# Weight splits held behind the residual chain, and three chain operations on another engine, in a two-layer hybrid trunk

## The chip, the cores and the metric

The kernel runs on one core of a Trainium2 chip. TensorE does the matrix products, VectorE and ScalarE the elementwise work, GpSimd some of it and a part of the DMA issues; SyncE (SP) issues the weight transfers. The metric is device time in microseconds of one execution; lower is better. Engine names in profiles: PE is TensorE (PEld its weight load), DVE is VectorE, ACT is ScalarE, POOL is GpSimd, SP is SyncE.

## What is computed

A decoder trunk of two layers on one sequence of 256 rows, 2048 wide, in float32. Each layer adds a normed mixer and a normed SwiGLU to the residual:

```python
def reference(x, mix_norm_pre, mix_norm_post, ffn_norm_pre, ffn_norm_post, ev_w_in, ...):
    h = x
    for layer in range(DEPTH):
        i = layer // 2
        u = rms_norm(h, mix_norm_pre[layer])
        if layer % 2 == 0:
            u = even_mixer(u, ev_w_in[i], ev_conv_w[i], ev_a_log[i], ev_dt_bias[i], ev_onorm[i], ev_w_out[i])
        else:
            u = odd_mixer(u, od_w_in[i], od_w_out[i])
        h = h + rms_norm(u, mix_norm_post[layer])
        u = swiglu(rms_norm(h, ffn_norm_pre[layer]), ffn_w_gate[layer], ffn_w_up[layer], ffn_w_down[layer])
        h = h + rms_norm(u, ffn_norm_post[layer])
    return h
```

`even_mixer` is one input projection, stick-breaking attention on 8 heads and gated DeltaNet on 8 others, and an output projection; `odd_mixer` has block-sparse and dilated attention between its two projections. The SwiGLU is 5632 wide.

## The kernel before

**Products.** The 256 rows are two tiles of 128, t = 0 and t = 1. A float32 product is three products of a reduced type: each operand is split into a high and a low part, and `step` (L271 to L273) adds high x high, high x low and low x high into the same PSUM tile. The activations are held transposed, one pair (high, low) per 512 columns. A step is 256 rows by 512 columns of a weight, with 6 matmuls for each tile.

**Weights.** All weights pass once through the chip. `load_until` (L230 on) issues a step's transfer on SP into one of four `raw` buffers (512 KB each), and `split` makes the parts: ScalarE copies the high one (L221), VectorE subtracts it for the low one (L222). Most steps have two halves of 128x512. A `raw` buffer is free for the next transfer when the splits have read it; the `w` pool holds ten steps. Some steps of the SwiGLU go a shorter way with sums of blocks (`split_sums`, `fast_step`); they aren't touched.

**Phases.** There are six: input projection, output projection and SwiGLU of each layer. In `run_phase` (L328), tile 0 runs up to eight steps ahead of tile 1 at a phase's beginning and end. When tile 0 has done its last step, `end(0)` writes its chain into the program, while TensorE goes on with tile 1's last steps:

- `post_residual` (L461): the factor `prf` from the sums of squares (`rms`, L205, with the power on GpSimd, L192, and L194, L198, L468), then for four column groups x += y * prf (L471) and the next phase's operand y (L475 behind the SwiGLU, L478 behind an output projection), which TensorE transposes (L373) and `split` divides into m tiles (L221, L222 again).
- The norm weights and y were multiplied before that: by L786 behind an output projection, by L731 in `down_chunk` behind the SwiGLU (column groups 0 to 2 on GpSimd, group 3 on VectorE). L722 adds the last product to y.

The chain has a raised priority (LEAD). The order on each engine is set by the scheduler of the language when the program is built, from the written order, priorities and its own estimate of when operands are ready; so the weight splits of the next phase are mixed with the chain on VectorE.

**DeltaNet.** `gdn_core` makes two 128-row blocks for each of two head groups. For each of the four, L1158 scales a product of keys into L, L1160 adds its two halves on GpSimd, and TensorE takes the sum into L1175. L1209 subtracts a state product on GpSimd (in two of the four).

Stages named in the text: A and B, two of the four L1160; F, G and H, the ends of layer 0's output projection, layer 0's SwiGLU and layer 1's output projection.

## Time and profile before

| | |
|---|---|
| Runs, us | 2388.26, 2392.54, 2393.22 (median 2392.54) |
| Profiled execution, us | 2395.03 |
| Its span, us | 2393.3 |
| Mean granted clock of TensorE | 0.99 |
| Busy: PE, PEld, DVE, ACT, POOL | 98%, 84%, 74%, 52%, 9% |

The span runs from the first to the last instruction; the execution's time has 1.7 us around it. The page gives shares over the whole span. With TensorE at 98%, what matters is where it is not busy, which the views by waits and by stretches show. The granted clock is the share of the full 2.4 GHz that TensorE was given; 0.5 is 1.2 GHz. Busy times of a group count overlapping parts of neighbouring instructions twice, so a pitch (start to start) is shorter than a mean duration.

### The profile page before, as it was taken

To read this page: it belongs to the slowest core of one execution; us is meant where nothing else is said; L and a number is where in the kernel's file an instruction comes from. 1 tells how busy PE (TensorE), PEld (TensorE's weight loads), DVE (VectorE), ACT (ScalarE), POOL (GpSimd) and SP (SyncE) were. 2 spreads that over 40 slices of the span, in tenths; PEclk is the share of its full clock that TensorE was granted. 3 is DMA by queue.
4 is the path that set the end of the run, shared out by engine and by line. 5 is a ranking of instruction groups with operands and counts; after the bars stand their busy time and mean duration, and the time that the engine had idled before them with its cause. 6 is when DMAs were issued, how large, how long until landed. Compare 5 with 4: busy or idle time off the path is not lost.

```text
span 2393.3 us, 33293 instructions
## 1 busy us (share of the span) xinstructions
PE 2346.8 (98%) x12235; PEld 2007.9 (84%) x12235; DVE 1760.4 (74%) x2823; ACT 1256.2 (52%) x1975; POOL 218.6 (9%) x269
## 2 busy tenths in 40 slices
PE   9999989999999999999998999999999999999998
PEld 7878877778888888888887888887888888888886
DVE  7775875668868697877867555567886878697885
ACT  6654564555645454544555545455554545454552
POOL 0430361210000000000121000011000000000011
PEclk9999999999999999999999999999999999999999
DMA  7644445365656556565675555576565656666573
GB/s 248 207 145 146 141 141 172 115 225 178 217 177 197 191 194 200 187 217 169 220 253 194 168 175 176 181 231 214 176 226 168 210 180 194 193 194 201 191 264 110
DMA packets 131140, 453.72 MB, mean 190 GB/s; under 512 B 15568, under 2 KB 20944, under 8 KB 130976
## 3 DMA queue, kind: packets, MB, share of 16 engines
q1 hardware_dynamic: 120704, 423.81, 53.9%
q0 software_dynamic: 8112, 26.52, 3.5%
q8 instruction: 96, 1.57, 0.3%
q10 hardware_dynamic: 2160, 1.27, 0.2%
q14 instruction: 68, 0.56, 0.1%
HBM read 443.11 MB, written 8.42 MB: 189 GB/s over the span
## 4 chain that ended last, share of the span: by engine, by line
PE 80%; DVE 3%; DMA 1%; issue 1%; POOL 1%; ACT 1%; DVEq 0%; POOLq 0%; ACTq 0%
PE p L273 11%; PE p L271 11%; PE p L272 11%; PE acc L273 10%; PE acc L271 10%; PE acc L272 10%; PE acc L296 2%; PE acc L297 2%; PE acc L295 2%; PE p L297 2%; PE p L296 2%; PE p L295 2%; DVE w L222 1%; PE p L216 1%; DMA raw<-in_ffn_w_down 1%
## 5 line engine op out<-in xcount | busy, mean ns | idle before, releaser
L222 DVE TENSOR_TENSOR w<-raw,w 128x512 fp32r<-128x512 f32 (+4 forms) x1104 | 987.2, 915 | 432.6 <-ACT w L221 386.6
L221 ACT ACTIVATE w<-raw 128x512 fp32r<-128x512 f32 (+4 forms) x1104 | 844.1, 795 | 832.5 <-PE p L273 313.7
L271 PE MATMUL acc<-w,m 128*128 128x512 f32 (+2 forms) x1582 | 617.4, 391 | 5.5 <-ACT m L224 3.2
L272 PE MATMUL acc<-w,m 128*128 128x512 f32 (+2 forms) x1582 | 616.4, 390 | 0.0
L273 PE MATMUL acc<-w,m 128*128 128x512 f32 (+2 forms) x1582 | 615.3, 390 | 0.8 <-DVE m L222 0.8
L271 PE MATMUL p<-w,m 128*128 128x512 f32 x1146 | 450.0, 393 | 3.6 <-ACT m L221 2.9
L273 PE MATMUL p<-w,m 128*128 128x512 f32 x1146 | 449.9, 393 | 0.0
L272 PE MATMUL p<-w,m 128*128 128x512 f32 x1146 | 449.3, 392 | 0.0
L271 PEld LDWEIGHTS acc<-w,m 128*128 128x128 f32 x1582 | 299.9, 190 | 64.9 <-ACT m L224 3.8
L273 PEld LDWEIGHTS acc<-w,m 128*128 128x128 f32 x1582 | 299.4, 189 | 61.1 <-DVE m L222 1.7
L272 PEld LDWEIGHTS acc<-w,m 128*128 128x128 f32 x1582 | 299.7, 189 | 57.4
L271 PEld LDWEIGHTS p<-w,m 128*128 128x128 f32 x1146 | 216.1, 189 | 48.0 <-ACT m L221 3.3
L273 PEld LDWEIGHTS p<-w,m 128*128 128x128 f32 x1146 | 215.7, 188 | 45.0
L272 PEld LDWEIGHTS p<-w,m 128*128 128x128 f32 x1146 | 215.8, 188 | 44.1
L222 DVE TENSOR_TENSOR w<-sums,w 128x1024 fp32r<-128x1024 f32 x126 | 153.5, 1218 | 3.0 <-ACT w L221 2.9
L221 ACT ACTIVATE w<-sums 128x1024 fp32r<-128x1024 f32 x126 | 132.4, 1051 | 18.8 <-DVE sums L259 18.5
L297 PE MATMUL acc<-w,m 128*128 128x256 f32 x462 | 131.5, 285 | 0.0
L296 PE MATMUL acc<-w,m 128*128 128x256 f32 x462 | 130.7, 283 | 0.0
L295 PE MATMUL acc<-w,m 128*128 128x256 f32 x462 | 130.5, 282 | 0.0
L257 DVE TENSOR_TENSOR sums<-raw 128x512 f32<-128x512 f32 x126 | 86.8, 689 | 51.1 <-DMA raw<-in_ffn_w_gate 25.4
L438 POOL DMA_DIRECT2D m<-in_ffn_norm_post x16 | 8.8, 551 | 1264.0 <-PE p L273 630.4
L297 PE MATMUL p<-w,m 128*128 128x256 f32 x420 | 119.3, 284 | 0.0
(279 smaller groups left out, 2372.1 us busy)
## 6 DMA issues: line engine op xcount, KB each, us to landing
raw<-in_ffn_w_gate SPq DMA_DIRECT2D x176, 512.0 KB, 3.5
raw<-in_ffn_w_up SPq DMA_DIRECT2D x176, 512.0 KB, 4.1
raw<-in_ffn_w_down SPq DMA_DIRECT2D x176, 512.0 KB, 4.5
raw<-in_ev_w_in SPq DMA_DIRECT2D x104, 512.0 KB, 3.5
raw<-in_od_w_in SPq DMA_DIRECT2D x96, 512.0 KB, 3.5
raw<-in_ev_w_out SPq DMA_DIRECT2D x32, 512.0 KB, 4.5
raw<-in_od_w_out SPq DMA_DIRECT2D x32, 512.0 KB, 4.5
xd<-m POOLq DMA_DIRECT2D x24, 256.0 KB, 4.0
```

The costliest lines, as they stand in the source:

```text
L216: self.nc.tensor.transpose(o[:, j * P:(j + 1) * P], src[:, j, :], self.ident)
L221: self.nc.scalar.activation(h, src, AF.Copy)
L222: self.nc.vector.tensor_sub(l, src, h.bitcast(F32))
L257: nc.vector.tensor_sub(t[:, 0:2], b[:, 0:1].broadcast_to([P, 2, 256]), b[:, 1:3])
L271: nc.tensor.matmul(acc, xh, s.wh[:, j], start=(s.first and j == 0), stop=False)
L272: nc.tensor.matmul(acc, xh, s.wl[:, j], start=False, stop=False)
L273: nc.tensor.matmul(acc, xl, s.wh[:, j], start=False, stop=end)
L295: nc.tensor.matmul(acc, xh, s.wh[:, b], start=s.first and i in (0, 2), stop=True, **kw)
L296: nc.tensor.matmul(acc, xh, s.wl[:, b], start=False, stop=True, **kw)
L297: nc.tensor.matmul(acc, xl, s.wh[:, b], start=False, stop=True, **kw)
L438: self.nc.gpsimd.dma_start(out=w, in_=src.broadcast_to([P, 512]))
```

## The change

1. `post_residual` returns its last VectorE operation, and `run_phase` keeps it together with the next four steps (HOLD) whose transfers haven't been issued. When `load_until` comes to these steps, the VectorE half of their splits (L222) is ordered behind that operation; the ScalarE half and the transfer aren't. That happens at the end of layer 0's output projection, layer 0's SwiGLU and layer 1's output projection; the input projections have no such chain, and behind the last SwiGLU no step is left.
2. L731 (column groups 0 to 2), L1160 and L1209 go from GpSimd to VectorE: 12, 4 and 2 instructions.

```diff
@@ -55,6 +57,7 @@
 PSA = 3
 NSP = 3
 LEAD = 500
+HOLD = 4
 PS_FFN = 3
 WARM = 10
 FFN_GROUPS = ((0, 1), (2, 3), (4, 5), (6, 7), (8, 9), (10,))
@@ -154,7 +157,7 @@
         psb = pool("psb", bufs=1, space=PSUM)
         dram = pool("dram", bufs=1, space=bass.MemoryType.DRAM)
         self.mem = Pool(big, "m", NTILES)
-        self.lag = LAG
+        self.lag, self.hold = LAG, None
         self.ps = Pool(psb, "p", NPS)
         self.pa = Pool(psb, "acc", PSA)
         self.cin = Pool(big, "c", 2, (P, 4, P + 3))
@@ -215,11 +218,12 @@
         for j in range(4):
             self.nc.tensor.transpose(o[:, j * P:(j + 1) * P], src[:, j, :], self.ident)
 
-    def split(self, h, l, src, scale=None):
+    def split(self, h, l, src, scale=None, after=None):
 
         if scale is None:
             self.nc.scalar.activation(h, src, AF.Copy)
-            self.nc.vector.tensor_sub(l, src, h.bitcast(F32))
+            with self.tc.issue_after(after) if after is not None else nullcontext():
+                self.nc.vector.tensor_sub(l, src, h.bitcast(F32))
         else:
             self.nc.scalar.activation(h, src, AF.Copy, scale=scale)
             self.nc.vector.scalar_tensor_tensor(l, src, scale, h.bitcast(F32), op0=ALU.mult, op1=ALU.subtract)
@@ -240,14 +244,18 @@
                                    for a in (raw, w[0][:, :1024], w[0][:, 1024:]))
                 nc.sync.dma_start(out=raw, in_=s.src)
                 if s.chunk.ffn:
-                    self.split(s.wh, s.wl, raw)
+                    self.split(s.wh, s.wl, raw, after=self.after(s))
                 else:
                     for j in range(2):
-                        self.split(s.wh[:, j], s.wl[:, j], raw[:, j])
+                        self.split(s.wh[:, j], s.wl[:, j], raw[:, j], after=self.after(s))
             else:
                 nc.sync.dma_start(out=raw, in_=s.src.rearrange("p k n -> p (k n)"))
                 self.split_sums(raw.rearrange("p (b n) -> p b n", b=4), s, *w)
             self.loaded += 1
+
+    def after(self, s):
+
+        return self.hold[1] if self.hold and s in self.hold[0] else None
 
     def split_sums(self, b, s, wh, wl):
 
@@ -343,7 +351,8 @@
                 self.step(0, self.steps[n0])
                 n0 += 1
                 if n0 == hi:
-                    end(0)
+                    done = end(0)
+                    self.hold = done and (self.steps[self.loaded:self.loaded + HOLD], done)
             else:
                 self.step(1, self.steps[n1])
                 n1 += 1
@@ -468,19 +477,20 @@
         nc.vector.tensor_mul(rf, r, f)
         for c in range(4):
             x, y = self.x[t][c], self.y[t][c]
-            nc.vector.scalar_tensor_tensor(x, y, rf, x, op0=ALU.mult, op1=ALU.add)
+            done = nc.vector.scalar_tensor_tensor(x, y, rf, x, op0=ALU.mult, op1=ALU.add)
             if then == "out":
                 nc.sync.dma_start(out=self.out[t * P:(t + 1) * P, c * 512:(c + 1) * 512], in_=x)
             elif then == "in":
-                nc.vector.tensor_mul(y, x, self.nwb[c])
+                done = nc.vector.tensor_mul(y, x, self.nwb[c])
                 self.aT[t].append(self.transposed(y))
             elif then == "ffn":
-                nc.vector.scalar_tensor_tensor(y, x, self.scale[t], self.nwb[c], op0=ALU.mult, op1=ALU.mult)
+                done = nc.vector.scalar_tensor_tensor(y, x, self.scale[t], self.nwb[c], op0=ALU.mult, op1=ALU.mult)
                 self.aT[t].append(self.transposed(y))
             if then != "ffn":
                 self.mem.give(y)
         if t == 1 and then != "out":
             self.mem.give(*self.nwb)
+        return done.ins
 
     def reload_x(self, t, src):
         self.x[t] = self.now(self.mem, 4)
@@ -728,16 +738,17 @@
             self.square_sum(y, self.yss[t][:, c:c + 1])
             w = self.now(self.mem)
             self.norm_weight(w, "ffn_norm_post", layer, c)
-            (nc.gpsimd if c < 3 else nc.vector).tensor_mul(w, y, w)
+            nc.vector.tensor_mul(w, y, w)
             self.mem.give(y)
             self.y[t][c] = w
 
     def end_ffn(self, t, layer):
         with self.tc.high_priority(offset=LEAD):
-            self.post_residual(t, "out" if layer else "in")
+            done = self.post_residual(t, "out" if layer else "in")
         if layer == 0:
             self.prenorm_factor(t)
             self.store_x(t)
+        return done
 
     def store_x(self, t):
         for c in range(4):
@@ -787,13 +798,14 @@
 
     def end_out(self, t, layer):
         with self.tc.high_priority(offset=LEAD):
-            self.post_residual(t, "ffn")
+            done = self.post_residual(t, "ffn")
         if t == 1:
             self.sums_of_tiles(self.y)
             for b in range(2):
                 self.mem.give(*self.y[b])
         self.prenorm_factor(t, True)
         self.store_x(t)
+        return done
 
 
     def attn_chunk(self, t, layer, g, kind, acc):
@@ -1157,7 +1169,7 @@
         for h in range(4):
             nc.vector.scalar_tensor_tensor(L[:, h], v4(o)[:, h], c2[:, h:h + 1], L[:, h],
                                            op0=ALU.mult, op1=ALU.mult)
-        nc.gpsimd.tensor_add(L_[:, :2 * P], L_[:, :2 * P], L_[:, 2 * P:])
+        nc.vector.tensor_add(L_[:, :2 * P], L_[:, :2 * P], L_[:, 2 * P:])
         self.ps.give(o)
         yield
         o = yield from self.ps.take()
@@ -1206,7 +1218,7 @@
             for h in range(4):
                 mm(v4(o)[:, h], kT[:, h], v4(self.state[g])[:, h], start=True, stop=True)
             nc.vector.tensor_mul(ks, v4(o), self.bc(c4))
-            nc.gpsimd.tensor_sub(B, B, ks)
+            nc.vector.tensor_sub(B, B, ks)
             self.ps.give(o)
             yield
             yield
```

The import of `nullcontext` is left out. Lines of the changed kernel are later: L222 becomes L226, L471 L480, L475 L484, L478 L487, L722 L732, L731 L741, L1160 L1172, L1158 L1170, L451 L460. VectorE has 18 instructions more and GpSimd 18 fewer; the order of SP is the same.

**VectorE at stage A** (`m_1334` is L, `w<-raw` a weight split). Before:

```order
L1165 TENSOR_TENSOR m_1394<-p_1563,gc_1510 128x512
L1248 TENSOR_TENSOR gcc<-gc_1512 128x4
L1158 SCALAR_TENSOR_TENSOR m_1334<-p_1537,gc_1511,m_1334 128x128 x4
L222 TENSOR_TENSOR w<-raw,w 128x512 x5
L1177 TENSOR_TENSOR m_1334<-p_1595,m_385 128x256
L222 TENSOR_TENSOR w<-raw,w 128x512
L1188 TENSOR_TENSOR m_1395<-m_1395,m_1334 128x64x2 x2
```

Now:

```order
L1177 TENSOR_TENSOR m_1394<-p_1563,gc_1510 128x512
L1260 TENSOR_TENSOR gcc<-gc_1512 128x4
L1170 SCALAR_TENSOR_TENSOR m_1334<-p_1537,gc_1511,m_1334 128x128 x4
L226 TENSOR_TENSOR w<-raw,w 128x512 x2
L1172 TENSOR_TENSOR m_1334<-m_1334 128x256
L226 TENSOR_TENSOR w<-raw,w 128x512 x4
L1189 TENSOR_TENSOR m_1334<-p_1595,m_385 128x256
L226 TENSOR_TENSOR w<-raw,w 128x512
L1200 TENSOR_TENSOR m_1395<-m_1395,m_1334 128x64x2 x2
```

The addition stands behind two of six weight splits; at B (`m_3165`) it stands right behind the four L1170.

**VectorE at stage F**, from `prf` to the first low half (m_4931) of a transposed tile; m_4328 to m_4331 are x, m_4344, m_4585, m_4765 and m_4906 are y. Before:

```order
L468 TENSOR_TENSOR prf<-pny,pna 128x1
L222 TENSOR_TENSOR w<-raw,w 128x512
...
L471 SCALAR_TENSOR_TENSOR m_4331<-m_4906,prf,m_4331 128x512
L222 TENSOR_TENSOR w<-raw,w 128x512 x2
L478 SCALAR_TENSOR_TENSOR m_4344<-m_4328,pscale,m_4336 128x512
L222 TENSOR_TENSOR w<-raw,w 128x512
...
L478 SCALAR_TENSOR_TENSOR m_4906<-m_4331,pscale,m_4339 128x512
L222 TENSOR_TENSOR w<-raw,w 128x512 x3
...
L222 TENSOR_TENSOR w<-raw,w 128x512 x2
...
L786 TENSOR_TENSOR m_5087<-acc_4991,m_5087 128x512
L222 TENSOR_TENSOR m_4931<-p_4925,m_4930 128x512
```

Now:

```order
L477 TENSOR_TENSOR prf<-pny,pna 128x1
L480 SCALAR_TENSOR_TENSOR m_4328<-m_4344,prf,m_4328 128x512
...
L480 SCALAR_TENSOR_TENSOR m_4331<-m_4906,prf,m_4331 128x512
L487 SCALAR_TENSOR_TENSOR m_4344<-m_4328,pscale,m_4336 128x512
...
L487 SCALAR_TENSOR_TENSOR m_4765<-m_4330,pscale,m_4338 128x512
L487 SCALAR_TENSOR_TENSOR m_4906<-m_4331,pscale,m_4339 128x512
L226 TENSOR_TENSOR w<-raw,w 128x512 x6
L208 TENSOR_SCALAR pj,pv<-xss 128x5
L226 TENSOR_TENSOR w<-raw,w 128x512 x2
L226 TENSOR_TENSOR m_4931<-p_4925,m_4930 128x512
```

Some rows, most of them of other column groups, are left out. Ten splits stood among and behind the chain; eight stand behind it now, and H reads the same.

**ScalarE at stage F** (m_5088 is tile 1's, its last square sum; m_4930 and m_4941 are high halves of tile 0's transposed y). Before:

```order
L221 ACTIVATE w<-raw 128x512 x2
L451 ACTIVATE m_4975,xss<-m_4331 128x512
L221 ACTIVATE w<-raw 128x512 x2
L451 ACTIVATE m_5088,xss<-acc_4991 128x512
L221 ACTIVATE m_4930<-p_4925 128x512
L221 ACTIVATE m_4941<-p_4936 128x512
L221 ACTIVATE w<-raw 128x512 x2
L221 ACTIVATE m_4952<-p_4947 128x512
```

Now:

```order
L460 ACTIVATE m_4973,xss<-m_4330 128x512
L460 ACTIVATE m_4975,xss<-m_4331 128x512
L224 ACTIVATE w<-raw 128x512 x2
L224 ACTIVATE m_4930<-p_4925 128x512
L224 ACTIVATE m_4941<-p_4936 128x512
L224 ACTIVATE m_4952<-p_4947 128x512
L224 ACTIVATE w<-raw 128x512
L224 ACTIVATE m_4963<-p_4958 128x512
L224 ACTIVATE w<-raw 128x512
L460 ACTIVATE m_5088,xss<-acc_4991 128x512
```

Tile 1's square sum came ahead of the high halves and now comes behind them.

**VectorE at stage G**, from `prf` to the first low half (m_11304); m_6338, m_6412 and m_6490 are tile 1's y. Before:

```order
L468 TENSOR_TENSOR prf<-pny,pna 128x1
L222 TENSOR_TENSOR w<-raw,w 128x512 x2
L722 TENSOR_TENSOR m_6338<-m_6338,p_11405 128x512
L471 SCALAR_TENSOR_TENSOR m_11208<-m_11226,prf,m_11208 128x512
...
L471 SCALAR_TENSOR_TENSOR m_11211<-m_11283,prf,m_11211 128x512
L222 TENSOR_TENSOR w<-raw,w 128x512 x3
L722 TENSOR_TENSOR m_6412<-m_6412,acc_11438 128x512
L222 TENSOR_TENSOR w<-raw,w 128x512
L475 TENSOR_TENSOR m_11226<-m_11208,m_11216 128x512
...
L475 TENSOR_TENSOR m_11283<-m_11211,m_11219 128x512
...
L222 TENSOR_TENSOR w<-raw,w 128x512 x2
L222 TENSOR_TENSOR m_11304<-p_11298,m_11303 128x512
```

Now:

```order
L477 TENSOR_TENSOR prf<-pny,pna 128x1
L741 TENSOR_TENSOR m_11395<-m_6264,m_11395 128x512
L480 SCALAR_TENSOR_TENSOR m_11208<-m_11226,prf,m_11208 128x512
...
L480 SCALAR_TENSOR_TENSOR m_11211<-m_11283,prf,m_11211 128x512
L484 TENSOR_TENSOR m_11226<-m_11208,m_11216 128x512
L732 TENSOR_TENSOR m_6338<-m_6338,p_11405 128x512
...
L484 TENSOR_TENSOR m_11283<-m_11211,m_11219 128x512
L226 TENSOR_TENSOR w<-raw,w 128x512 x8
L732 TENSOR_TENSOR m_6412<-m_6412,acc_11438 128x512
L741 TENSOR_TENSOR m_11428<-m_6338,m_11428 128x512
...
L732 TENSOR_TENSOR m_6490<-m_6490,acc_11471 128x512
L226 TENSOR_TENSOR m_11304<-p_11298,m_11303 128x512
```

Some rows are left out again. The splits have left the chain for a place behind it, ahead of the first low half; two L741 that GpSimd had stand here too.

## Rows read from the trace of the kernel before

**Rows 1.** The page: busy time of each engine, share, instructions.

```profile
PE 2346.8 (98%) x12235; PEld 2007.9 (84%) x12235; DVE 1760.4 (74%) x2823; ACT 1256.2 (52%) x1975; POOL 218.6 (9%) x269
```

**Rows 2.** Waits of TensorE: total us, times, longest us.

```profile
PE p L1175 <- POOL m L1160: 9.3, 2, 6.0
PE p L373 <- DVE m L475: 4.9, 1, 4.9
...
PE p L271 <- ACT m L221: 2.9, 1, 2.9
...
PE acc L271 <- ACT m L221: 2.3, 2, 1.2
```

**Rows 3.** TensorE by stretches: length, busy (matmuls), PEclk, DMA share, GB/s.

```profile
140.00:150.00 10.00, 6.74 (x26) 0.83 0.54 163
...
344.00:360.00 16.00, 9.96 (x37) 0.79 0.44 143
...
530.00:540.00 10.00, 8.42 (x33) 0.83 0.79 260
...
1256.00:1284.00 28.00, 20.00 (x84) 0.82 0.56 193
...
1658.00:1668.00 10.00, 7.84 (x39) 1.00 0.79 241
```

**Rows 4.** Timeline of A and B: GpSimd and VectorE (start, length).

```profile
141.06 2.31 POOL L1160 TENSOR_TENSOR m<-m 128x256 f32<-128x256 f32 x1 [2.41 <-DVE m L1158]
...
342.20 1.82 POOL L1037 TENSOR_TENSOR m<-m,le_anti 128x512 f32<-128x512 f32 x1
...
342.79 1.26 DVE L197 TENSOR_TENSOR gra<-gra,gss 128x8 f32<-128x8 f32 x1
...
346.94 3.09 DVE L222 TENSOR_TENSOR w<-raw,w 128x512 fp32r<-128x512 f32 x5
...
347.11 3.51 POOL L1160 TENSOR_TENSOR m<-m 128x256 f32<-128x256 f32 x1 [3.09 <-DVE m L1158]
```

**Rows 5.** Stage F: VectorE by lines, 520.3 to 531.7; then timelines.

```profile
L222 DVE TENSOR_TENSOR w<-raw,w 128x512 fp32r<-128x512 f32 x10 | 6.5, 684 | 0.0
...
520.94 2.73 DVE L471 SCALAR_TENSOR_TENSOR m<-m,prf,m 128x512 f32<-128x512 f32 x4
...
527.99 0.74 DVE L478 SCALAR_TENSOR_TENSOR m<-m,pscale,m 128x512 f32<-128x512 f32 x1
...
532.42 0.68 DVE L222 TENSOR_TENSOR m<-p,m 128x512 fp32r<-128x512 f32 x1
...
531.92 0.50 PE L271 MATMUL acc<-w,m 128*128 128x512 f32 x1 [1.09 <-ACT m L221]
...
544.30 0.74 DVE L478 SCALAR_TENSOR_TENSOR m<-m,pscale,m 128x512 f32<-128x512 f32 x1
...
547.15 2.24 PE L373 MATMUL p<-ident,m 128*128 128x128 f32 x19
```

**Rows 6.** Stage G: VectorE by lines, 1247.2 to 1263.8; timelines; DMA issues.

```profile
L222 DVE TENSOR_TENSOR w<-raw,w 128x512 fp32r<-128x512 f32 x12 | 9.0, 773 | 0.4 <-ACT w L221 0.4
...
1252.16 0.15 DVE L468 TENSOR_TENSOR prf<-pny,pna 128x1 f32<-128x1 f32 x1
...
1254.03 3.77 DVE L471 SCALAR_TENSOR_TENSOR m<-m,prf,m 128x512 f32<-128x512 f32 x4
...
1260.29 5.26 POOL L731 TENSOR_TENSOR m<-m,m 128x512 f32<-128x512 f32 x1 [1.37 <-DVE m L722]
...
1261.55 1.94 PE L373 MATMUL p<-ident,m 128*128 128x128 f32 x8 [4.93 <-DVE m L475]
...
1267.90 1.27 DVE L222 TENSOR_TENSOR m<-p,m 128x512 fp32r<-128x512 f32 x2
...
1271.65 2.74 DVE L471 SCALAR_TENSOR_TENSOR m<-m,prf,m 128x512 f32<-128x512 f32 x4
...
raw<-in_od_w_in SPq DMA_DIRECT2D x14, 512.0 KB, 4.3
```

More of the change, by code (lines that the diff above doesn't have):

```diff
@@ L24 @@
+from contextlib import nullcontext
 import numpy as np
```

## The prediction

> **What bounds the kernel now.** I read the page's busy times first [rows 1]: TensorE is busy for 2346.8 of 2393.3 us, so the change can win only what TensorE stands idle, 46.5 us in all, and what its clock loses around that. Next came the waits of TensorE [rows 2], to see which idle the change can touch: 9.3 us in two waits (the longest 6.0) on the GpSimd addition L1160, 4.9 us on L475, which closes the residual chain of the first row tile at the end of layer 0's SwiGLU, and 2.9 and 2.3 us on the high parts of transposed tiles behind such chains. Then the busy time by stretches [rows 3]. Idle is the length less PE busy; the clock's loss is the length times (1 - PEclk), where the granted clock drops from 2.4 to 1.2 GHz for a while behind some pauses:
>
> A (DeltaNet, 140 us): idle 3.26, clock 1.7. B (DeltaNet, 344 us): 6.04 and 3.4. F (end of layer 0's output projection): 1.58 and 1.7. G (end of its SwiGLU): 8.00 and 5.0. H (end of layer 1's output projection): 2.16 and 0.
>
> That is 21.0 us idle and 11.8 us of clock, the ceiling of the whole change. The rest of the idle (start, other DeltaNet waits, the tail) has no part in it.
>
> **The moved additions (A and B).** In B five weight splits (L222) run on VectorE back to back from 346.94, 3.09 us long, so 0.62 each; L1160 is recorded from 347.11 for 3.51 us, to 350.62, half a microsecond beyond the last of them [rows 4]. In A it ends at 143.37. So the addition is not long work; it waits while VectorE splits. On VectorE I cost it at half of a 128x512 split, an estimate of 0.35 us.
> - A: the changed order has it behind two splits. Its inputs are there by 141.0 (L1160 is recorded from 141.06), so it ends about 141.0 + 1.2 + 0.35 = 142.55, against 143.37: 0.8 us. Two matmuls of weight steps (0.4 us, as the page's 2346.8 us for 12235 matmuls make 0.19 each) also come ahead of the waiting product. Gain 1.2 us. Lower bound -0.4, if the next GpSimd operation, freed from its place behind L1160, is in the way first.
> - B: it stands right behind the products that feed it, so TensorE could go on at 347.3 instead of 350.67, a gain of 3.2. But the next 128x512 operation of GpSimd now comes some 3 us earlier, amid VectorE's short operations, and such a meeting has a price: L197, on 128x8, took 1.26 us beside L1037, which itself took 1.82 [rows 4]. I take 1.2 us off: 2.0, with 3.2 as the upper bound.
>
> Here the Trainium skill speaks against the change. The rows first: an operation of GpSimd beside splits runs to the end of the splits, and a tiny VectorE operation beside one of GpSimd takes as long as a large one. "SBUF — State Buffer", in "SBUF: two separate sides", has the rule: a VectorE operation with two inputs in SBUF and one of GpSimd exclude each other, and whichever starts first holds the ports to its end. The trace agrees in both directions. By the rule the moved addition could be the one shut out, in A (-0.4) as in B (2.0), and the whole sum would be 11.1 us instead of 12.7.
>
> I take A at 1.2 because its addition now follows two splits without a gap, which is the situation in which the rows show GpSimd shut out. Clock in A and B: 5.1 us are lost today, but a pause of one to three microseconds stays in both, so I count nothing back; 5.1 is the upper bound.
>
> The subtraction L1209 and the products L731 are the other moved operations. The former has no matmul waiting in the rows above: 0. The latter matter in G.
>
> **The held splits in F and H.** From the factor prf to the first low half of the transposed tile VectorE has no idle [rows 5]: ten splits of next-phase weights (10 x 0.60 = 6 us) are mixed with eight chain operations. Without them the chain takes 8 x 0.66 = 5.3 us (the pitch of the four L471, 2.73 us with their overlap) from 520.35, one split ahead of 520.94; so it ends at 525.65 instead of 528.73. The eight held splits then take 4.9 us, to 530.6, and the low half is written by 531.3 instead of 533.1 (532.42 + 0.68). TensorE stands ready at 530.83 (531.92 - 1.09) and reads the low half first in the third product, some 0.4 us later, so this is just in time. The high half on ScalarE, which ended the wait of 1.09, stands behind a square sum L451 of the other tile before, and ahead of it in the changed order. So F's 1.58 go, and as no pause is left, its clock loss of 1.7 too: 3.3 us. H has the same sequence with 2.16 us and no clock: 2.2 us. Bounds: 0 for both, if the held splits end just later than I add up; 5.5 is also the upper bound.
>
> The held splits are the same work, 0.4 to 5 us later, so the second tile's chain is not delayed in sum: VectorE has no idle there in either order. Its last operation in F ends at 545.04 (544.30 + 0.74) and the transposes that need it start at 547.15 [rows 5], a cover of 2.1 us. Matmuls that come 1.6 us earlier use up most of it; were it gone, each microsecond of delay would cost one.
>
> **G.** Here the chain starts at 1247.2 and ends at 1263.8; twelve splits, 9.0 us, lie inside it [rows 6], and GpSimd works beside it on L731: the four L471 take 3.77 us, where the second tile's four, alone, take 2.74. A clean chain, by that second tile, takes twice this less an overlap, 5.2 us. Four of the twelve splits lie ahead of prf (1252.16), at 0.77 a mean one; without them I set prf at 1249.1. With 0.75 for prf and one moved L731, 5.2 for the chain and 0.6 for one addition in it, the chain ends at about 1255.7, 8.1 us earlier. TensorE ends the second tile's steps only at 1256.62 (1261.55 - 4.93), so the 4.9 us wait goes. Then comes the new wait: the first low half (today from 1267.90 to 1268.58) stands behind eight held splits (to 1260.6) and some 1.6 us of additions, a moved L731 and a norm operation; it is written about 1262.9. TensorE, through sixteen transposes at 1258.5 (nineteen take 2.24 us [rows 5]) and two products 0.4 us later, will idle some 4 us for it. The low half comes 1268.6 - 1262.9 = 5.7 us earlier, and the matmuls with it. Since a pause remains, I leave one more spell at half clock behind it, worth 1.7 as in F: gain **4.0**. Bounds: 9.0, if all of the 13.0 us of idle and clock were saved but the 4; 2.0 from below, if the next loads give some back. SP issues a transfer when a raw buffer is freed, by a split: now by the held ones, 1256.3 to 1260.6, where the splits inside the chain freed them from 1248 on. The last of these transfers lands 4.3 us later [rows 6], at 1265; the first step that needs one is the seventh, 36 matmuls of 0.19 us behind 1262.9, so at 1269.7. I count nothing.
>
> **The sum.** 1.2 + 2.0 + 3.3 + 4.0 + 2.2 = 12.7 us, from the profiled execution's 2395.03 to 2382.3. That execution is 2.5 us above the median of the runs (2392.54), so against the median the forecast is 2392.5 - 12.7 = **2379.8 us**. A change of 0.2% is 4.8 us, about what a measurement of this kernel can tell from none.
>
> **Rivals.**
> 1. *Given back.* The hold frees raw buffers late, so SP issues later, and TensorE waits for weights at the start of the next phase; or the remaining pauses cost clock as before. For it: in G the buffers come free up to 8 us later, and the low half waits behind all eight splits. Against it: F and H have covers. G then gives 2.0, F 1.6 without its clock, A and B together 2.0, H 1.2: 6.8 us, 2385.7 (2383 to 2388).
> 2. *It doesn't do what it says.* The scheduler fills the places with other VectorE work, such as the second tile's additions or the splits of transposed tiles, and the moved additions meet GpSimd's next operation; gains and losses of 1 to 2 us cancel. For it: in G the order still has two L722 and a norm operation between. Against it: in F and H nothing but the chain stands there. Within 4.8 us of 2392.5.
> 3. *Slower.* The chain isn't shortened, because its operations wait for something else than the splits ahead of them (a square sum, the GpSimd power, a transpose's PSUM tile), while the eight held splits now stand between chain and low halves. Point of decision: the chain in F must end by 527.5 for the low half to be no later than today's 533.1. If it ends at 528.7 as today, the low half comes 528.7 + 4.9 + 0.7 = 534.3 instead of 533.1: 1.2 us lost in F, 1.2 in H; in G the chain's end at 1263.8 + 4.9 + 1.6 + 0.7 = 1271.0 against 1268.6, 2.4 lost, and one more half-clock spell, 1.7: together 6.5 us, 2399. Against it: VectorE shows no idle in F and H between prf and the low half, so the queue alone is what the chain waits for.
>
> **How the numbers follow.** Forecast (2371 to 2383): 0.53. Rival 1: 0.25. Rival 2: 0.12. Rival 3: 0.06. Better than 2371, the upper bounds of several terms and the clock of A and B too: 0.04. All of the forecast, the better case and nearly all of rival 1 are faster by over 4.8 us: 0.80. Same: rival 2 and the slow edge of rival 1, 0.14. Slower 0.06. The range 2371 to 2388 holds the forecast and rival 1.
>
> **What would show it.** Right: the waits on L1172 (L1160 before) shrink from 9.3 to 4 to 5 us; no L226 on a weight stands between prf and the chain's last operation, eight stand behind; in F and H TensorE has no gap over 0.3 us and the clock in F stays at 2.4 GHz; in G the wait for L484 is gone and one of 3 to 4 us for the low half stands in its place. Wrong: the same gaps in F and H under another name; a new wait of TensorE for weights within 20 us after the chains; the second tile's transposes starting after a pause; VectorE waiting in the GDN stage where GpSimd waited.

## The result, and the profile after

The changed kernel takes 2381.89 us (median of 4 runs, 2379.59 to 2382.66) against 2392.88 us (4 runs, 2388.26 to 2396.07): ratio 0.9948, 95% interval 0.9936 to 0.9960, so 12.4 us faster by the ratio and 11.0 by the medians. The profiled executions stand at 2381.79 and 2395.03, 13.2 us apart. The forecast was 2379.8, inside a range of 2371 to 2388.

The page of the changed kernel, its busy times; they answer to [rows 1]:

```profile
PE 2342.9 (98%) x12235; PEld 2004.3 (84%) x12235; DVE 1765.3 (74%) x2841; ACT 1255.9 (53%) x1975; POOL 190.1 (8%) x251
```

VectorE has 18 instructions more and is busy 4.9 us longer, although 18 operations at 0.4 to 0.7 us each came over. The last experiments take that up again.

The waits of TensorE (total, times, longest), which answer to [rows 2]:

```profile
PE p L1187 <- DVE m L1172: 6.3, 2, 4.2
PE p L382 <- DVE m L226: 4.4, 1, 4.4
...
PE acc L279 <- ACT m L224: 0.7, 2, 0.4
```

The two waits on the DeltaNet addition fell from 9.3 to 6.3 us. The waits on L475 and on the high half behind it (4.9 and 2.9) became one of 4.4, on the low half L226. The 2.3 us on high halves in F and H are gone (the two of together 0.7 in the last line lie between 400 and 515 us); H keeps two waits of 0.3 us on low halves.

TensorE by stretches, in the columns of [rows 3]: A, B, F, G and H, each moved to where the stage now lies:

```profile
140.00:150.00 10.00, 7.96 (x39) 1.00 0.47 153
342.00:358.00 16.00, 11.79 (x53) 0.89 0.51 164
522.00:532.00 10.00, 9.92 (x52) 1.00 0.72 237
1248.00:1276.00 28.00, 23.30 (x105) 0.88 0.58 198
1646.00:1656.00 10.00, 9.71 (x50) 1.00 0.83 279
```

Idle (length less busy) went from 3.26 to 2.04 in A, 6.04 to 4.21 in B, 1.58 to 0.08 in F, 8.00 to 4.70 in G, 2.16 to 0.29 in H. The granted clock is full in A and F now. For the sum, I numbered the 12235 matmuls of both traces by their start and took the difference of the starts of equal numbers; so each stage shows what it moved, idle and clock together:

| matmul number | start before, us | after minus before, us | between: |
|---|---|---|---|
| 60 | 17.1 | +1.0 | the start |
| 780 | 152.5 | -1.1 | A: -2.1 |
| 1440 | 274.5 | -1.4 | |
| 1800 | 356.4 | -4.2 | B: -2.8 |
| 2280 | 449.2 | -4.4 | |
| 2820 | 571.2 | -7.9 | F: -3.5 |
| 6600 | 1288.4 | -11.2 | G: -3.3 |
| 8520 | 1690.0 | -13.4 | H: -2.1 |
| last | | -13.4 | |

The start (first weights and the constants' transfers) is not touched by the change; in the traces of the runs below it varies by up to 3 us in the first 100. So a single microsecond of the whole time says nothing, but the places do. A difference takes in all that lies between its two points: A by itself is -2.5 (the shift is +1.5 at matmul 490, ahead of it), and G by itself -3.8 (the shift is -7.4 at matmul 6400).

VectorE in F, from `prf` to the held splits, in the changed kernel:

```profile
515.82 0.16 DVE L477 TENSOR_TENSOR prf<-pny,pna 128x1 f32<-128x1 f32 x1
516.02 2.74 DVE L480 SCALAR_TENSOR_TENSOR m<-m,prf,m 128x512 f32<-128x512 f32 x4
518.67 2.73 DVE L487 SCALAR_TENSOR_TENSOR m<-m,pscale,m 128x512 f32<-128x512 f32 x4
521.33 3.09 DVE L226 TENSOR_TENSOR w<-raw,w 128x512 fp32r<-128x512 f32 x5
```

The chain takes 5.4 us, from 516.02 to 521.40 (8.4 before [rows 5]), and the splits follow. The wait in front of TensorE's first product [rows 5] has no successor.

VectorE in G, and TensorE beside it:

```profile
1241.65 0.15 DVE L477 TENSOR_TENSOR prf<-pny,pna 128x1 f32<-128x1 f32 x1
1241.77 0.69 DVE L741 TENSOR_TENSOR m<-m,m 128x512 f32<-128x512 f32 x1
1242.38 2.73 DVE L480 SCALAR_TENSOR_TENSOR m<-m,prf,m 128x512 f32<-128x512 f32 x4
...
1246.23 1.89 DVE L484 TENSOR_TENSOR m<-m,m 128x512 f32<-128x512 f32 x3
1248.04 4.89 DVE L226 TENSOR_TENSOR w<-raw,w 128x512 fp32r<-128x512 f32 x8
...
1254.13 0.68 DVE L732 TENSOR_TENSOR m<-m,acc 128x512 f32<-128x512 f32 x1
1254.73 1.28 DVE L226 TENSOR_TENSOR m<-p,m 128x512 fp32r<-128x512 f32 x2
```

```profile
1250.64 0.40 PE L280 MATMUL p<-w,m 128*128 128x512 f32 x1
1255.47 1.12 PE L382 MATMUL p<-ident,m 128*128 128x128 f32 x4 [4.43 <-DVE m L226]
1256.23 0.78 PE L281 MATMUL p<-w,m 128*128 128x512 f32 x1
```

The chain is done at 1248.1. The first low half starts at 1254.73, behind eight held splits, three operations of 0.68 us and a norm operation, and TensorE has done two products and stands until 1255.47 for it.

### The profile page after: what moved, and what is told of

The parts are those of the page before. It is cut to its first block, busy times and chain, and to the rows that moved or that the text cites. A ratio compares the mean times of both kernels' runs of the same rounds, so it can differ in the third digit from the quotient of the medians.

```text
span 2379.9 us, 33308 instructions
## 1 busy us (share of the span) xinstructions
PE 2342.9 (98%) x12235; PEld 2004.3 (84%) x12235; DVE 1765.3 (74%) x2841; ACT 1255.9 (53%) x1975; POOL 190.1 (8%) x251
## 4 chain that ended last, share of the span: by engine, by line
PE 77%; DVE 2%; issue 1%; DMA 1%; ACT 0%; POOL 0%; DVEq 0%; POOLq 0%; ACTq 0%
PE p L281 11%; PE p L279 11%; PE p L280 11%; PE acc L281 10%; PE acc L279 10%; PE acc L280 10%; PE acc L304 2%; PE acc L305 2%; PE acc L303 2%; PE p L304 2%; PE p L305 2%; PE p L303 2%; PE p L219 1%; DVE w L226 1%; DMA raw<-in_ffn_w_down 0%
## 5 line engine op out<-in xcount | busy, mean ns | idle before, releaser
L226 DVE TENSOR_TENSOR w<-raw,w 128x512 fp32r<-128x512 f32 (+4 forms) x1104 | 982.4, 912 | 424.2 <-ACT w L224 374.8
L226 DVE TENSOR_TENSOR w<-sums,w 128x1024 fp32r<-128x1024 f32 x126 | 153.4, 1218 | 3.2 <-ACT w L224 3.1
L305 PE MATMUL p<-w,m 128*128 128x256 f32 x420 | 119.3, 284 | 0.0
L303 PE MATMUL p<-w,m 128*128 128x256 f32 x420 | 119.0, 283 | 0.0
```

The costliest lines, as they stand in the source:

```text
L226: self.nc.vector.tensor_sub(l, src, h.bitcast(F32))
L303: nc.tensor.matmul(acc, xh, s.wh[:, b], start=s.first and i in (0, 2), stop=True, **kw)
L305: nc.tensor.matmul(acc, xl, s.wh[:, b], start=False, stop=True, **kw)
```

## The experiments

Two parts were taken apart first, then the place of the hold was varied, then the remaining wait in B was followed to its cause. Every ratio below is to the kernel before, run beside it on the same chip (medians 2395.13, 2396.08 and 2396.26 us in the three groups of runs). Ratios are compared, not medians.

**The hold alone.**

```diff
-            nc.vector.tensor_mul(w, y, w)
+            (nc.gpsimd if c < 3 else nc.vector).tensor_mul(w, y, w)
-        nc.vector.tensor_add(L_[:, :2 * P], L_[:, :2 * P], L_[:, 2 * P:])
+        nc.gpsimd.tensor_add(L_[:, :2 * P], L_[:, :2 * P], L_[:, 2 * P:])
-            nc.vector.tensor_sub(B, B, ks)
+            nc.gpsimd.tensor_sub(B, B, ks)
```

> The hold alone; L731, L1160 and L1209 are back on GpSimd. My theory (the hold and the moved additions win in different stages and add up): in F and H TensorE has no gap over 0.3 us, as with the whole change; in A and B the waits on the GpSimd addition are back, 3.3 and 6.0 us; G has one wait of 4 to 5 us and not two of 4.9 and 2.9. The two additions were worth 2.1 + 2.8 = 4.9 us by the shift between the two traces, so the time is 2381.9 + 4.9 = 2386.8, between 2385 and 2389. Rival (the products L731 on VectorE shorten G's chain, and not the hold): G keeps over 7 us of waits, and the time is 2390 to 2392.

2387.02 us, ratio 0.9961 (0.9948 to 0.9973). By the time alone this run and the whole change aren't clearly apart, as the two intervals overlap by half; the places tell them apart. The waits of TensorE in this run:

```profile
PE p L1187 <- POOL m L1172: 9.3, 2, 6.0
PE p L382 <- DVE m L226: 4.4, 1, 4.4
```

A and B wait as before, F and H have no gap over 0.3 us, and G has the one wait of 4.4 of the whole change. By the matmul numbers F moves by -3.5 us and G by -3.4. So the hold carries F, G and H, and the products L731 nothing of G: the rival falls. On GpSimd (L741 in this kernel) they do lengthen G's chain, in which the four L480 take 3.81 us here and 2.73 in the whole change; but then the two that VectorE had there, of 0.6 us each, are not in its queue, and the low half comes no later.

**The moved operations alone.** `HOLD = 4` becomes `HOLD = 0`.

> HOLD = 0: no split is held, the 18 operations are on VectorE. My theory: A and B as with the whole change (waits of 2.0 and 4.2 us); F keeps 1.6 us of waits, H 2.2, G 7 to 8; time 2392.9 - 4.9 = 2388, between 2386 and 2390. Rival (products): G falls to about 4 us of waits without the hold, and the time is 2384 to 2386. Second rival (only a reshuffled order brings the gain, from either part alone): F and H lose their waits here too, 2382.

2391.81 us, ratio 0.9983 (0.9974 to 0.9992), 4.1 us by the ratio. Its stretches A, B, F, G and H:

```profile
140.00:150.00 10.00, 7.96 (x32) 0.83 0.57 190
342.00:358.00 16.00, 11.79 (x51) 0.79 0.51 164
526.00:536.00 10.00, 8.41 (x35) 0.83 0.78 256
1252.00:1280.00 28.00, 20.88 (x87) 0.82 0.56 190
1654.00:1664.00 10.00, 8.50 (x44) 1.00 0.78 252
```

Idle in A and B is that of the whole change to a hundredth, in F that of before, in G 7.1 of 8.0, in H 1.5 of 2.2. The time lies above the 2386 to 2390 that I expected, as those were set against a base of 2392.9; against this group's 2395.1 the expected gain of 4.9 us lies inside the interval (1.9 to 6.2 us). The parts add up: 0.39% and 0.17% make 0.56%, and the whole has 0.52%.

**The addition alone.**

```diff
-HOLD = 4
+HOLD = 0
-            nc.vector.tensor_mul(w, y, w)
+            (nc.gpsimd if c < 3 else nc.vector).tensor_mul(w, y, w)
-            nc.vector.tensor_sub(B, B, ks)
+            nc.gpsimd.tensor_sub(B, B, ks)
```

> Only the addition L1160 is on VectorE; nothing is held, L731 and L1209 are on GpSimd. My theory: A and B as with the whole change, all else as before, time 2388, within 1 us of the run with all three moved. Rival (the products or the subtraction win or lose something by themselves): 2 to 4 us off that run, with the difference in G or behind 420 us.

2391.08 us, ratio 0.9979 (0.9971 to 0.9988). That is the run of all three moves within its interval, so the four additions carry what the 18 moved operations bring; the 12 products and 2 subtractions show no effect of their own that these intervals (2 us to either side) could tell.

**The low halves ahead of the held splits.** In G, `post_residual` returns the low half of the second transposed column group:

```diff
-                self.nc.vector.tensor_sub(l, src, h.bitcast(F32))
+                self.low = self.nc.vector.tensor_sub(l, src, h.bitcast(F32))
...
-                done = nc.vector.tensor_mul(y, x, self.nwb[c])
+                nc.vector.tensor_mul(y, x, self.nwb[c])
                 self.aT[t].append(self.transposed(y))
+                first = self.low if c < 2 else first
+                done = first
```

> The whole change, but at the end of layer 0's SwiGLU the four steps are held behind the first two low halves of the transposed tile and not behind the chain's last product. My theory (the 4.4 us that TensorE still waits in G are the eight held splits that stand ahead of the first low half): that wait falls to under 1 us, nothing else changes, time 2381.9 - 3.5 = 2378.4, up to 2 us better still if the half clock behind it goes, between 2376 and 2380. Rival (raw buffers freed 1 to 3 us later starve the phase that follows): a wait for weights of 2 to 4 us appears within 20 us behind the chain, and the time stays at 2381 to 2383.

2379.11 us, ratio 0.9932 (0.9919 to 0.9944). Stretch G, and TensorE there:

```profile
1248.00:1276.00 28.00, 25.92 (x121) 1.00 0.67 230
```

```profile
1253.37 0.50 PE L279 MATMUL p<-w,m 128*128 128x512 f32 x1 [0.25 <-ACT m L224]
1254.32 0.66 PE L382 MATMUL p<-ident,m 128*128 128x128 f32 x4 [0.22 <-DVE m L226]
```

The 4.43 us are 0.22 now, the clock stays full, and idle in the stretch is 2.1 in place of 4.7. So it was the splits ahead of the low half that TensorE stood for. One wait of 1.1 us is new, on the second tile's L484; the second tile's chain now binds there. By the ratios the version is 0.16% better than the whole change, and the two intervals overlap by a third of their length; the places show it more plainly than the time: between the matmuls of the table G moves by -7.2 us in place of -3.3.

**A hold of two steps.** `HOLD = 4` becomes `HOLD = 2`.

> HOLD = 2 in place of 4, all else as in the whole change. In F and H the scheduler's order around the chain is then the same; in G three splits stand in the chain again, and five in place of eight behind it, so the same number of splits stands ahead of the first low half. My theory (what counts is how much VectorE work stands ahead of the first low half, and the chain's own end only where the transposes wait for it): no change, a wait of 4 to 5 us in G, time within 1.5 us of the whole change beside the same runs of before, ratio 0.993 to 0.996. Rival (the chain's end counts): 1.8 us more in G.

2382.28 us, ratio 0.9943 (0.9931 to 0.9955), with a wait of 4.44 us in G. No change, although three splits stand in G's chain again: how many operations stand ahead of the low half decides, not in which order.

**A hold behind the last low half, in all three places.**

```diff
-                done = nc.vector.tensor_mul(y, x, self.nwb[c])
+                nc.vector.tensor_mul(y, x, self.nwb[c])
                 self.aT[t].append(self.transposed(y))
+                done = self.low
...
-                done = nc.vector.scalar_tensor_tensor(y, x, self.scale[t], self.nwb[c], op0=ALU.mult, op1=ALU.mult)
+                nc.vector.scalar_tensor_tensor(y, x, self.scale[t], self.nwb[c], op0=ALU.mult, op1=ALU.mult)
                 self.aT[t].append(self.transposed(y))
+                done = self.low
```

> The whole change, but everywhere the four steps are held behind the last low half of tile 0's transposed tiles. In the order of VectorE at G all held splits then stand behind the second tile's chain too, about 10 us later than in the whole change. My theory (a hold gives back what it wins as soon as weights come later than TensorE's need; the third step's weights are due 3 us after the phase begins): the wait for the first low half in G goes (4.4 us), a wait for weights of 6 to 9 us comes in its place, 4 us slower than the whole change, ratio 0.995 to 0.998; F and H gain or lose under 1 us. Rival (there is slack in the weights, the low halves are all that counts): faster than the whole change by 3 us or more, ratio 0.991 to 0.993.

2388.26 us, ratio 0.9970 (0.9959 to 0.9981): slower than the whole change by 0.22%, as I expected, but elsewhere. (Its interval and that of the whole change meet, at 0.9959 and 0.9960; that of the hold of two steps, run beside it, lies apart.) Waits of TensorE:

```profile
PE p L280 <- DVE w L226: 2.9, 3, 2.1
PE p L382 <- DVE m L484: 2.5, 1, 2.5
PE acc L280 <- DVE w L226: 2.4, 2, 2.1
```

The two of 2.1 us on a weight's low half (L226 w) are in F and H, in F 19 us behind the chain's end, and each is followed by a spell at half clock (PEclk 0.83 over 10 us in both places, 1.00 in the changed kernel). By the matmul numbers F and H first win 3 to 4 us and then give back some 6 each, while G by itself moves by -6.1 us (-3.8 in the whole change). In G the wait for weights that I had expected (6 to 9 us) did not come, though the held splits stand behind the second tile's L480 there; what remains is 2.5 us on that tile's L484. So the mechanism was right (a hold that lasts too long comes back as a wait for weights), and the place was wrong: it is F and H that have no slack for it.

**What is left in B.** The wait of 4.2 us lies behind this chain of the changed kernel; GpSimd beside it in the second fence:

```profile
339.46 1.24 DVE L199 TENSOR_TENSOR gra<-gry 128x8 f32<-128x8 f32 x1 [1.83 <-POOL gry L195]
...
341.23 1.26 DVE L200 TENSOR_TENSOR gra<-gra,gss 128x8 f32<-128x8 f32 x1
342.41 0.68 DVE L226 TENSOR_TENSOR w<-raw,w 128x512 fp32r<-128x512 f32 x1
343.01 1.26 DVE L201 TENSOR_SCALAR gra<-gra 128x8 f32<-128x8 f32 x1
...
346.61 0.42 DVE L1172 TENSOR_TENSOR m<-m 128x256 f32<-128x256 f32 x1
```

```profile
340.64 1.82 POOL L1049 TENSOR_TENSOR m<-m,le_anti 128x512 f32<-128x512 f32 x1
342.98 1.26 POOL L1134 TENSOR_TENSOR m<-m,onorm 128x512 f32<-128x512 f32 x1 [0.52 <-ACT m L1129]
```

L199, L200 and L201, on 128x8, each take 1.24 to 1.26 us beside an operation of GpSimd; L201 ends when L1134 does. With L1134 on VectorE:

```diff
-        nc.gpsimd.tensor_mul(zw, zw, self.rep(self.onorm))
+        nc.vector.tensor_mul(zw, zw, self.rep(self.onorm))
```

> The whole change, and L1134 (the output norm's product of 128x512 in the DeltaNet blocks, four times) goes from GpSimd to VectorE. In the whole change L201 on 128x8 takes 1.26 us beside L1134 in the chain ahead of B. My theory (the remaining 4.2 us of B hold this one collision): L201 takes 0.16 us, the wait in B falls from 4.2 to about 3.1 us, 1 us faster, up to 3 with a shorter spell at half clock: ratio 0.992 to 0.995. Rival (L201 is long for another reason, or L1134 itself now stands in the chain): the wait stays at 4 us or grows.

2378.64 us, ratio 0.9927 (0.9915 to 0.9940). The interval still touches that of the whole change (by 0.0004); of the runs beside it, all five (2377.42 to 2379.93) are faster than all five of the hold of two steps (2381.58 to 2384.04). The chain in this run:

```profile
339.62 1.25 DVE L199 TENSOR_TENSOR gra<-gry 128x8 f32<-128x8 f32 x1 [1.54 <-POOL gry L195]
...
341.40 0.15 DVE L200 TENSOR_TENSOR gra<-gra,gss 128x8 f32<-128x8 f32 x1
341.59 0.17 DVE L201 TENSOR_SCALAR gra<-gra 128x8 f32<-128x8 f32 x1
```

L201 takes 0.17 us in place of 1.26, and the wait in B is 1.8 us, not 3.1 (the two on L1172 make 3.9, the longest 2.1): the scheduler also left one split out between L200 and L201, and L1049 now meets L199 instead of L200, so that one of the three is long and not all. The collision that the edit was made for is 1.1 of the 2.4 us by which the wait fell; the rest came with the changed order. "SBUF — State Buffer" of the Trainium skill, in "SBUF: two separate sides", states that an operation of GpSimd excludes one of VectorE with two inputs in SBUF or in a two-port mode, whichever starts first. The trace agrees, with 1.26 against 0.15 us for L200, which has two inputs, and 1.26 against 0.17 for L201; L201 has one input, and in which mode it ran no run here shows.

**Both products, with and without the low halves first.** L1049 goes to VectorE as well:

```diff
-            nc.gpsimd.tensor_mul(v22(E), v22(E), mask)
+            nc.vector.tensor_mul(v22(E), v22(E), mask)
```

> The whole change with both L1134 and L1049 on VectorE, the four steps held behind the chain's last product as in the change (so without the low halves first). My theory (the two moves and the low halves first add up, as they act in different stages): A and B as in the run with all three, waits of 1 to 2 us there and no spell at half clock behind A; G keeps its wait of 4.4 us; 3 us slower than that run: ratio 0.990 to 0.992. Rival (the three moves only help together): at the time of the version with L1134 alone, ratio 0.9927 or above.

2374.44 us, ratio 0.9907 (0.9891 to 0.9924). As expected, the two waits for the addition are 1.2 and 1.1 us, no half-clock spell follows A, and G keeps its wait of 4.4.

> The version with the low halves first in G, and both L1134 and L1049 (the decay mask's product, 128x512) on VectorE. My theory: no operation of GpSimd stands beside the chain ahead of B, L200 and L201 take 0.16 us each, L1049 itself adds 0.6 us to the chain and the two splits ahead of L1172 1.2 us; the wait in B is 3 to 4 us; A as before or 1 us worse; time 1 us below the version with the low halves first, ratio 0.991 to 0.994. Rival (VectorE, busy without a gap there, pays for each moved operation what the collision cost): no gain over that version, or 1 to 3 us worse.

2371.03 us, ratio 0.9897 (0.9884 to 0.9910). The waits for the addition in that run (its lines stand two further down: L1172 is L1174, L1049 L1051, L1134 L1136):

```profile
PE p L1189 <- DVE m L1174: 2.3, 2, 1.2
```

From 6.3 to 2.3 us, although the addition stands behind two splits in B too, where I had expected 3 to 4 us and 1.1 are left. L201 takes 0.16 us, but L200 does not: in A and in B it still stands beside a convolution sum of GpSimd that began ahead of it (in B from 336.08, 1.70 us long).

```profile
336.55 1.25 DVE L200 TENSOR_TENSOR gra<-gra,gss 128x8 f32<-128x8 f32 x1
```

My expectation for the time was too low: I allowed 1 us of gain over the version with the low halves first (0.9932), and it was 0.35%, 8 us. The low halves first bring 0.10% here and 0.16% without the two moves, so the edits add up as far as the intervals allow.

**The convolution's 28 operations as well.** All L1093 and L1095 (16 products and 12 sums of 128x512) go to VectorE:

```diff
-                nc.gpsimd.tensor_mul(v4(a), c[:, :, j:j + P], self.bc(w[:, :, j]))
+                nc.vector.tensor_mul(v4(a), c[:, :, j:j + P], self.bc(w[:, :, j]))
...
-                    nc.gpsimd.tensor_add(nat, nat, tmp)
+                    nc.vector.tensor_add(nat, nat, tmp)
```

> The version with all three, and the 28 products and sums of the short convolution of v (L1093, L1095 in the changed kernel) on VectorE too, 0.6 us each, 17 us in all. My theory (a moved operation wins only where a chain with TensorE behind it runs beside GpSimd; elsewhere it delays weight splits): L200, which still takes 1.25 us beside such a sum, falls to 0.16, worth 1 us at most; 17 us more on VectorE, which is busy without a gap for stretches there, cost 0 to 4 us; ratio 0.989 to 0.992, no better than without. Rival (each GpSimd operation shuts VectorE out for about its own length, so each move wins): 3 us or more faster, ratio below 0.9885.

2366.46 us, ratio 0.9875 (0.9860 to 0.9890): 0.22% better than without, beyond what I expected, and in the rival's range (the two runs are of different groups, and their intervals overlap by 0.0006). The 28 operations, 19.3 us of work, cost VectorE next to nothing. Page of the run ahead of it, then of this one:

```profile
PE 2341.7 (99%) x12235; PEld 2001.9 (84%) x12235; DVE 1767.5 (74%) x2853; ACT 1258.1 (53%) x1975; POOL 165.8 (7%) x239
```

```profile
PE 2336.0 (99%) x12235; PEld 1998.7 (85%) x12235; DVE 1769.4 (75%) x2881; ACT 1256.8 (53%) x1975; POOL 145.0 (6%) x211
```

The first is the run with all three edits. VectorE is busy 1.9 us longer with 28 more operations. The weight splits of 60 to 420 us show where their time comes from, in the same order:

```profile
L226 DVE TENSOR_TENSOR w<-raw,w 128x512 fp32r<-128x512 f32 x196 | 141.8, 760 | 58.8 <-ACT w L224 58.0
```

```profile
L226 DVE TENSOR_TENSOR w<-raw,w 128x512 fp32r<-128x512 f32 x198 | 132.6, 703 | 46.9 <-ACT w L224 45.2 <-PE acc L280 1.2
```

Two more splits, 9.2 us less: the mean falls from 760 to 703 ns, that of a split without company being 684 [rows 5]. The 14 operations L199 and L200 in the same stretch give another 6 us, from 8.4 to 2.4; L200 at B now reads:

```profile
331.88 0.17 DVE L200 TENSOR_TENSOR gra<-gra,gss 128x8 f32<-128x8 f32 x1
```

So most of what the moved operations take on VectorE is time that it had stood beside GpSimd before. In this run TensorE has no gap over 0.3 us between 91 and 388 us; the waits for the addition (1.2 and 1.1 us) and one of 0.5 are gone.

Where TensorE won that time is a narrower question. By the matmul numbers the two traces are 8.1 us apart at the end: 1.7 at 92 us, ahead of the first of the moved operations (112 us), where the run without them has a half-clock spell and this one none; 3.4 more up to 450 us; and 3.0 behind that, where none of them lies. Of the 3.4, 2.8 are the waits just named, which stand behind chains that TensorE waits for; so my theory of where a move wins is not refuted. Its prices were wrong: more than the 1 us that I allowed for the chains, and nothing to be seen of the 0 to 4 us on the splits. This kernel is the fastest of those run; against the changed kernel, 0.9875 to 0.9948, it is 0.73% ahead.

## Why the prediction was right

It was right in its direction, its size and in most of its places. By step:

- **F, 3.3 us.** Measured 3.5. The chain ended 3 us earlier as worked out (5.4 us long for 5.3), the low halves came in time, and as no pause was left the clock stayed full: PEclk 1.00 for 0.83 before. The hold alone gives the same 3.5.
- **H, 2.2 us.** Measured 2.1. But only 1.5 of the 2.16 us idle before are F's sequence; 0.68 were a wait for the high half of a weight (L221 w, at 1665.33 us), for which the prediction had no reason. It is gone in the runs of either part alone too, so this much of the agreement is luck.
- **G, 4.0 us.** Measured 3.3. The chain and the place of the new wait came out as the order of VectorE gave them: "some 4 us" of idle for the low half behind eight splits, 4.43 in the trace. The rival version with the low halves first shows that this wait was the splits' alone. The term is 0.7 above the measured 3.3, but 0.5 of that was lost between F and G (-7.9 at matmul 2820, -7.4 at 6400). G by itself moves by 4.7 us (-12.1 at 6540), and 0.9 of that are given back at the second tile (-11.2 at 6600), which the sum counted at nothing.
- **A, 1.2 us, and B, 2.0 us.** Measured 2.1 and 2.8. Idle fell by 1.22 and 1.83, as the two terms say to within 0.2. What the sum left out is the clock: I counted nothing back because a pause stays, but A has no half-clock spell in this trace and B a shorter one (PEclk 0.89 for 0.79). In the run with the moves alone, with the same idle, A's spell is there (0.83). So this part comes and goes with the same pause, and it can't be promised. The case of -0.4, in which the moved addition is shut out, didn't come: it took 0.41 us in A, and it was GpSimd's next operation that was shut out (5.13 us, below). One reading behind A was too broad, that an operation of GpSimd beside splits runs to their end. That holds in B; in A the addition ended at 143.37, amid five splits that took 4.70 us there and 3.09 in B:

```profile
140.91 4.70 DVE L222 TENSOR_TENSOR w<-raw,w 128x512 fp32r<-128x512 f32 x5
```

- **The meeting with GpSimd's next operation** in B was set at 1.2 us. It came in that size: L201 took 1.26 us beside L1134, and 0.17 without.
- **L1209**, at 0, and L731, whose move was to give G its clean chain: the run with the addition alone matches that with all three moves, and the hold without them has the same G. L731 did slow the chain by 1.1 us from GpSimd, and takes as much on VectorE.
- **The three rivals.** Giving back was the nearest: it took 0.9 us in G. How it would take more is shown by the hold behind the last low half, 0.22% worse than the change. The change does do what it says; and the chain waited for the queue alone, since with the splits gone from it, it shrank to the length of its eight operations.

The sum of the measured stages, 13.8 us, less 1.0 of the start and with 0.6 between the stages, is the 13.4 us by which the last matmul is earlier, against 12.7 forecast. That the two are so close is partly luck: A and B came out 1.7 us above the sum, by clock that it left out, and G 0.7 below it. That the median moved by 11.0 to 12.4 and not by 13.4 is within what executions of each kernel differ (8 us between the lowest and highest of before).

A flaw of the working remains: the ceiling of 11.8 us of clock counts each half-clock spell at half its length, though in G and B a part of it fell into TensorE's pauses, where a clock costs nothing. It entered the ceiling and the upper bounds (5.1 for A and B, 9.0 for G), but no term of the sum: the spell of F, whose 1.7 stands in F and G, began behind the pauses.

## What to carry to other kernels

Work that is queued between the links of a chain costs the chain its whole length, and held behind it costs only what stands ahead of the next thing that TensorE reads; so look at the first operand behind the chain, put that ahead of the held work too, and check that the next phase's first weights still come in time before holding for longer. An elementwise operation on GpSimd beside a busy VectorE is not free: here VectorE lost to it from half of the time that it would have spent on it (the 18 operations of the change: 11 us of work, 4.9 more busy) to nine tenths (the convolution: 19.3 and 1.9). Moves off GpSimd won some 0.2% of the time each where a chain that TensorE waits for ran beside it (L1160, L1134, L1049, the convolution), and showed no loss elsewhere (L731, L1209); single steps of that size are at the edge of what these runs can tell. Count the moved operation against the stretched ones beside it, not against VectorE's busy time.

## What the runs showed of the hardware that was not expected

- A GpSimd operation beside a row of splits is stretched far beyond its work: L1134 took 1.26 us in B and 5.13 in A of the changed kernel, where six splits and the addition ran back to back beside it, and a split behind them took 1.45 in place of 0.68. In the run of the hold alone, a product L741, 1.29 us long elsewhere in G, took 7.07 beside the eight held splits:

```profile
142.42 5.13 POOL L1134 TENSOR_TENSOR m<-m,onorm 128x512 f32<-128x512 f32 x1 [2.30 <-ACT m L1129]
```

```profile
146.65 1.45 DVE L226 TENSOR_TENSOR w<-raw,w 128x512 fp32r<-128x512 f32 x1
```

```profile
1253.78 7.07 POOL L741 TENSOR_TENSOR m<-m,m 128x512 f32<-128x512 f32 x1 [1.05 <-DVE m L732]
```

- Moving 28 operations of 128x512 on to an engine that was 74% busy raised its busy time by 1.9 us. "Perfetto Trace Analysis" of the Trainium skill, in "Optimizing Scalar/DVE Operations", says that offloading between GpSimd and VectorE might not help, as they share a port; here the way back from GpSimd helped by 0.20% to 0.22% a step (L1134, L1049, the convolution).
- The same pause can be followed by a half-clock spell or not: 2.04 us in A of the changed kernel was followed by none, and 2.04 us in A of the run with the moves alone by one (PEclk 1.00 and 0.83 in the same stretch). The pause of the kernel before in A, 3.3 us, came back in the run of the hold alone, at 0.66 in place of 0.83. What tells these apart was not tried.
